# All matrices B of the gates' expansion on VectorE instead of one in four on GpSimd

## The chip, the cores and the metric

The kernel runs on one core of one Trainium2 chip. The metric is the device time of one execution in microseconds (us). The core has a matrix engine (TensorE, PE in the profile, with its weight loads as PEld), VectorE (DVE), ScalarE (ACT), GpSimd (POOL) and SyncE (SP). Each of them works through its own queue of instructions in order, and waits on semaphores for the others. DMAs are issued by SP and, for gathers with an index per row, by POOL.

## The reference, cut to what matters

The block has two mixers side by side (a chunkwise mLSTM and a forgetting attention), an output projection, and then a product-key expert retrieval (PEER) over 16384 experts. It is the last part that the change is in. For each token and each of 8 heads it takes the 16 best of 128 x 128 experts, makes a softmax gate of their scores, and computes

```
u = u_emb[ids]                                   # 128 rows of 1024 for each token
act = gelu(einsum('ted,td->te', u, xb))
w = gate * act
out = einsum('te,ted->td', w, v_emb[ids])
```

So each token has 128 pairs (expert, gate); there are 1024 tokens and 128 experts' rows of u and of v for each of them.

## The kernel before, in words

The 1024 tokens are four segments of 256. The mixers run over the segments one after the other, each merged with the projections of the next segment and the expert choice (`topk`) of earlier ones. The expert sums are computed in two ways:

- **Segments 0 and 3 by gathers.** For each block of 128 tokens, POOL issues one indirect DMA for each of the 128 choices of rows of u (L325, tile `gu`, 128 rows of 4 KB). Each such tile is multiplied with the tokens and summed, on VectorE (L334), or, for 5 of 16 choices, multiplied on POOL (L331) and summed on ScalarE (L332). Then come 128 gathers of v (L361, tile `gv`), one for each token; after every fourth of them TensorE multiplies the four tiles with the gates (L383, `po`). The gathered tiles of segment 0 come from a pool of four buffers (GATH = 4), so a round of four `gv` has to be used by `po` before the next round can be issued. The four blocks' gathers stand in the order u of block 0, then v of block 0 and u of block 1 in turns of four, then v of block 1. For segment 3 they are paced: each is asked for at a fixed place in the dense stage, waits for TensorE's work up to there, and is used five steps later (`Paced`, L1005), so VectorE's, ScalarE's and TensorE's instructions that use it have fixed places among those of the dense stage.
- **Segments 1 and 2 densely.** For 512 tokens the scores with all 16384 experts are made with matmuls (`du` L289), passed through gelu, multiplied with a dense gate matrix and multiplied with all of v (`vo` L1222). Operands of these matmuls are split into a high and a low half: ScalarE casts (`wh` L277), VectorE subtracts (`wl` L282, some of them on POOL, L280, in earlier stages).

The dense gate matrix is made in `gates` (L1091), from the choices of segments 1 and 2, for each of 512 tokens: a matrix A (128 x 128) is one where the high part of a choice's id equals the column, a matrix B is the gate where the low part equals the column, and the product of B and A, a matmul over the 128 choices, is the token's gates for all 16384 experts (`gout` L1136). Tokens are taken four at a time; there are 128 such quads. In a quad, VectorE makes three A with one instruction (L1126), ScalarE the fourth with two (L1129, L1130); then four instructions at L1134 make the four B, then four matmuls, and ScalarE copies the result out of PSUM (L1138). A and B have two buffers each, the PSUM bank two. After eight quads SP writes 2 MB to DRAM (L1140). The line that changes chose POOL for the first B of a quad (GPOOL = 1) and VectorE for the other three.

This expansion is one of three generators that run merged (L1167): the expert choice of segment 3, the last 12 of 48 early blocks of dense scores (`spill`), and the gates. The gathers of segment 0 come later in program order (`gather_first(5)`, L1169), but the framework places each engine's instructions by a simulated timeline when it builds the program, so they stand between the others on POOL, from 383 us on. After the expansion its buffers are given up, and the dense stage takes their place. `po` matmuls and `gout` matmuls both have high priority in that placement. Once built, each engine's order is fixed.

Of the kernel before, what the change touches and what calls it, by code (L numbers as in the profile page):

```python
# [14 lines left out]
OP = mybir.AluOpType  # L15
# [41 lines left out]
SW = 1  # L57
GP0 = 5
GACT = 1
GPOOL = 1  # L60
T3W = 1.2
GW = 1
T00 = 0
# [28 lines left out]
def _block_kernel(ctx, tc, nc, I, out, dbg):  # L92
# [27 lines left out]
    def bank(name):  # L120
        turn_b[0] += 1
        if extra is not None and turn_b[0] % XB == 0:
            return extra[:, turn_b[0] // XB % 2, :]
        return ps.tile([P, 512], F32, tag="bank", name=name, bufs=2)
# [9 lines left out]
    dve, act, pe, pool_e, sync = nc.vector, nc.scalar, nc.tensor, nc.gpsimd, nc.sync  # L134
# [34 lines left out]
    iota = cp.tile([P, P], F32, tag="iota", name="iota")  # L169
# [921 lines left out]
    def gates(S, gb):  # L1091

        for b in range(NB):
            hi = gb.tile([P, P], I32, tag="gi", name="gi_hi")
            lo = gb.tile([P, P], I32, tag="gi", name="gi_lo")
            dve.tensor_scalar(hi, S.idx[:, b, :], 7, None, op0=OP.logical_shift_right)
            dve.tensor_scalar(lo, S.idx[:, b, :], 127, None, op0=OP.bitwise_and)
            T = []
            for x, nm in ((hi, "iT"), (lo, "jT"), (None, "gT")):
                if x is None:  # L1100
                    f = S.gate[:, b, :]
                else:
                    f = gb.tile([P, P], F32, tag="gf", name="gf", bufs=1)
                    dve.tensor_copy(f, x)
                tb = bank("gtr")
                with tc.high_priority():
                    pe.transpose(tb[:, 0:P], f, ident)
                t_ = gb.tile([P, P], F32, tag=nm, name=nm, bufs=1)
                act.copy(t_, tb[:, 0:P])
                T.append(t_)  # L1110
            iT, jT, gT = T
            if GACT:
                niT = gb.tile([P, P], F32, tag="niT", name="niT", bufs=1)
                act.mul(niT, iT, -1.0)
            for tg in range(P // TG):
                G = gb.tile([P, P, TG], F32, tag="G", name="G")
                for q in range(TG // 4):
                    bk = dps.tile([P, 512], F32, tag="db", name="gout")
                    t0 = tg * TG + q * 4
                    ts4 = slice(t0, t0 + 4)  # L1120
                    A = gb.tile([P, 4, P], F32, tag="A", name="A")
                    B = gb.tile([P, 4, P], F32, tag="B", name="B")
                    bc = [P, 4, P]
                    io = iota.unsqueeze(1).broadcast_to(bc)
                    nd = 4 - GACT
                    dve.tensor_tensor(A[:, 0:nd], io[:, 0:nd], iT[:, t0:t0 + nd].unsqueeze(2).broadcast_to([P, nd, P]),  # L1126
                                      op=OP.is_equal)
                    for u in range(nd, 4):
                        act.activation(A[:, u, :], iota, AF.Abs, bias=niT[:, t0 + u:t0 + u + 1])  # L1129
                        act.activation(A[:, u, :], A[:, u, :], AF.Relu, bias=1.0, scale=-1.0)  # L1130
                    for u in range(4):
                        t1 = slice(t0 + u, t0 + u + 1)
                        e = pool_e if u < GPOOL else dve
                        e.tensor_scalar(B[:, u, :], iota, jT[:, t1], gT[:, t1], op0=OP.is_equal, op1=OP.mult)  # L1134
                        with tc.high_priority():
                            pe.matmul(bk[:, u * P:(u + 1) * P], B[:, u, :], A[:, u, :], start=True, stop=True)  # L1136
                    with nullcontext():
                      act.copy(G[:, :, q * 4:q * 4 + 4].rearrange("p i t -> p t i"),  # L1138
                             bk.rearrange("p (t i) -> p t i", t=4))
                sync.dma_start(gd[(NB * (S.sg - DENSE[0]) + b) * (P // TG) + tg], G)  # L1140
                yield
# [21 lines left out]
    def all_gates():  # L1163
        for d in DENSE:
            yield from gates(segs[d], gb)
# [121 lines left out]
```

## Time and profile before

| what | value |
|---|---|
| median of 3 runs | 3746.05 us (3735.21 to 3759.56) |
| the profiled execution's own time | 3742.05 us |
| its span in the profile | 3740.3 us |
| busy share of the span | PE 81%, DVE 69%, POOL 52%, ACT 38% |
| stretch in which L1134 runs | 1699 to 2111 us |
| POOL's instructions at L1134 | 128, mean 1108 ns |
| VectorE's instructions at L1134 | 384, mean 398 ns |

The shares are averages over stages with different limits, so most of what follows is read from stretches of the span: which engine is busy in one, what the others wait for, and which of these waits ends last.

### The profile page before, as it was taken

The numbers are of one execution on the slowest core, as the hardware profiler recorded it, in microseconds if no ns is written. First come the engines' busy times: TensorE is split into PE (matmuls) and PEld (weight loads), VectorE is DVE, ScalarE is ACT, GpSimd is POOL, SyncE is SP. The second block draws the span as 40 slices with busy tenths as digits, with TensorE's granted clock in tenths as the row PEclk, the third lists the DMA queues.
The fourth block names the chain that finished last, engine by engine and source line by source line (L and its number), as shares of the span: only waits on it lengthen the run. The fifth ranks groups of instructions, "written<-read, shape, count | busy, mean of one in ns | idle before, by whom it ended". The sixth has DMA issues, their size and how long they took to land. (4 is left out here: it accounts for less than half of the span.)

```text
span 3740.3 us, 47105 instructions
## 1 busy us (share of the span) xinstructions
PE 3040.7 (81%) x15233; PEld 2324.6 (62%) x15233; DVE 2581.1 (69%) x6272; ACT 1435.7 (38%) x2915; POOL 1944.4 (52%) x1575
## 2 busy tenths in 40 slices
PE   7798776657778889887886599865798888989999
PEld 6686666446556667656765476644576555666667
DVE  6566999987447988888997443877655656654434
ACT  4565443345343323335655432322333332332222
POOL 3121566666545545557656422888655555543430
PEclk9899876768788999988998899887899999999999
DMA  4455577777877778767776777988888788889983
GB/s 140 123 156 166 191 228 243 240 226 250 229 241 238 242 223 257 240 239 263 271 251 234 272 253 248 325 285 287 283 295 293 269 284 290 313 317 328 330 292 109
DMA packets 375899, 931.54 MB, mean 249 GB/s; under 512 B 59316, under 2 KB 145556, under 8 KB 373604
## 3 DMA queue, kind: packets, MB, share of 16 engines
q0 software_dynamic: 161216, 552.56, 44.3%
q1 hardware_dynamic: 214436, 375.97, 30.4%
q8 instruction: 120, 1.97, 0.2%
q14 instruction: 127, 1.04, 0.1%
HBM read 860.91 MB, written 67.47 MB: 248 GB/s over the span
## 5 line engine op out<-in xcount | busy, mean ns | idle before, releaser
L282 DVE TENSOR_TENSOR wl<-raw,wh 128x512 fp32r<-128x512 f32 x736 | 608.4, 833 | 508.6 <-ACT wh L277 455.7
L277 ACT CAST wh<-raw 128x512 fp32r<-128x512 f32 x896 | 543.0, 617 | 971.4 <-DMA raw<-in_peer_v 208.5
L325 POOL DMA_INDIRECT gu<-in_peer_u,idx x512 | 578.9, 1131 | 567.9 <-PE po L383 173.7
L361 POOL DMA_INDIRECT gv<-in_peer_v,idT x512 | 558.2, 1090 | 603.4 <-PE po L383 198.2
L334 DVE SCALAR_TENSOR_TENSOR gu<-gu,xng 128x1024 f32<-128x1024 f32 x352 | 512.8, 1467 | 99.0 <-DMA gu<-in_peer_u,idx 91.9
L1222 PE MATMUL vo<-wh,Wh 128*128 128x512 f32 x1024 | 395.1, 418 | 138.5 <-ACT wh L277 114.0
L1222 PE MATMUL vo<-wl,Wh 128*128 128x512 f32 x1024 | 423.1, 413 | 12.2 <-DVE wl L282 12.1
L331 POOL TENSOR_TENSOR gu<-gu,xng 128x1024 f32<-128x1024 f32 x160 | 389.7, 2436 | 71.8 <-DMA gu<-in_peer_u,idx 66.3
L1222 PE MATMUL vo<-wh,Wl 128*128 128x512 f32 x1024 | 415.8, 408 | 0.0
L280 POOL TENSOR_TENSOR wl<-raw,wh 128x512 fp32r<-128x512 f32 x160 | 217.8, 1361 | 325.9 <-ACT wh L277 294.7
L1222 PEld LDWEIGHTS vo<-wh,Wh 128*128 128x128 f32 x1024 | 198.4, 197 | 231.9 <-ACT wh L277 136.3
L383 PE MATMUL po<-gv,Z 128*32 128x512 f32 x2048 | 273.4, 641 | 78.0 <-DMA gv<-in_peer_v,idT 78.0
L332 ACT ACTIVATE gu<-gu 128x1024 f32<-128x1024 f32 x160 | 169.2, 1058 | 364.6 <-POOL gu L331 357.2
L289 PE MATMUL du<-xh,wh 128*128 128x512 f32 x640 | 259.0, 405 | 30.3 <-ACT wh L277 30.3
L289 PE MATMUL du<-xh,wl 128*128 128x512 f32 x640 | 258.8, 405 | 22.2 <-DVE wl L282 22.1
L289 PE MATMUL du<-xl,wh 128*128 128x512 f32 x640 | 256.2, 400 | 0.0
L1222 PEld LDWEIGHTS vo<-wl,Wh 128*128 128x128 f32 x1024 | 204.0, 199 | 69.9 <-DVE wl L282 19.8
L1222 PEld LDWEIGHTS vo<-wh,Wl 128*128 128x128 f32 x1024 | 203.3, 199 | 51.9 <-issue 6.7
L1136 PE MATMUL gout<-A,B 128*128 128x128 f32 x1024 | 161.3, 310 | 65.1 <-POOL B L1134 51.9
L1136 PEld LDWEIGHTS gout<-A,B 128*128 128x128 f32 x1024 | 146.6, 217 | 93.8 <-POOL B L1134 69.9
L1227 DVE TENSOR_TENSOR acc<-acc,vo 128x512 f32<-128x512 f32 x256 | 164.7, 680 | 47.2 <-PE vo L1222 46.7
L1207 DVE TENSOR_TENSOR Wl<-w,Wh 128x512 fp32r<-128x512 f32 x128 | 96.0, 754 | 133.2 <-ACT Wh L1206 113.5
(431 smaller groups left out, 6696.3 us busy)
## 6 DMA issues: line engine op xcount, KB each, us to landing
raw<-in_ut SPq DMA_DIRECT2D x128, 512.0 KB
raw<-in_peer_v SPq DMA_DIRECT2D x256, 256.0 KB
raw<-in_wf SPq DMA_DIRECT2D x64, 512.0 KB
gd<-G SPq DMA_DIRECT2D x16, 2048.0 KB
Gt<-gd SPq DMA_DIRECT2D x32, 1024.0 KB
raw<-in_wt SPq DMA_DIRECT2D x48, 512.0 KB
raw<-in_wq SPq DMA_DIRECT2D x48, 512.0 KB
raw<-in_wo SPq DMA_DIRECT2D x32, 512.0 KB
```

The source lines that it names most:

```text
L277: act.copy(h, part)
L280: pool_e.tensor_sub(l, part, h.bitcast(F32))
L282: seen["dve"] = dve.tensor_sub(l, part, h.bitcast(F32))
L289: seen["pe"] = pe.matmul(o, w, x[:, c], start=(first and i == 0), stop=(last and i == 2))
L325: d = pool_e.indirect_dma_start(out=t, out_offset=None, in_=I["peer_u"], in_offset=bass.IndirectOffsetOnAxis(ap=S.idx[:, lb, r:r + 1], axi ...
L331: pool_e.tensor_tensor(t, t, xn[0], op=OP.mult)
L332: act.activation(t, t, AF.Copy, accum_out=G.actv[:, r:r + 1])
L334: dve.scalar_tensor_tensor(t, t, 1.0, xn[0], op0=OP.mult, op1=OP.mult, accum_out=G.actv[:, r:r + 1])
L361: d = pool_e.indirect_dma_start(out=t, out_offset=None, in_=I["peer_v"], in_offset=bass.IndirectOffsetOnAxis(ap=S.idT[lb][:, tok:tok + 1], ...
L383: last = pe.matmul(G.po[32 * q_:32 * q_ + 32, n, :], z[:, q_, 31 - j:63 - j], rows[q_][:, n * 512:(n + 1) * 512], start=(j == 0), stop=(j ...
L1136: pe.matmul(bk[:, u * P:(u + 1) * P], B[:, u, :], A[:, u, :], start=True, stop=True)
L1222: seen["pe"] = pe.matmul(bks[b], w[:, cw], v, start=(ii == 0 and i == 0), stop=(ii == GRP - 1 and i == 2))
```

## The change

The constant goes, and with it the choice of the engine: the first B of each quad is made by VectorE too, with the same instruction on the same operands.

```diff
-GPOOL = 1
...
                     for u in range(4):
                         t1 = slice(t0 + u, t0 + u + 1)
-                        e = pool_e if u < GPOOL else dve
-                        e.tensor_scalar(B[:, u, :], iota, jT[:, t1], gT[:, t1], op0=OP.is_equal, op1=OP.mult)
+                        dve.tensor_scalar(B[:, u, :], iota, jT[:, t1], gT[:, t1], op0=OP.is_equal, op1=OP.mult)
```

128 instructions move from POOL's queue to VectorE's. No DMA, no matmul and no buffer is added or taken away.

## Rows read from the trace of the kernel before

**Rows 1.** The page's 40 slices of 93.5 us: busy tenths of PE.
```profile
PE   7798776657778889887886599865798888989999
```
**Rows 2.** Stretches: from:to, length, busy us (instructions) by engine, PE clock, DMA share, GB/s.
```profile
1695.00:1965.00 270.00, 234.91 (x1496) 190.00 (x1500) 249.71 (x907) 158.67 (x322) 182.31 (x153) 0.93 0.72 255
1965.00:2115.00 150.00, 100.73 (x641) 77.87 (x633) 102.21 (x343) 87.54 (x185) 99.14 (x94) 0.85 0.62 230
...
2165.00:2365.00 200.00, 192.42 (x925) 141.19 (x925) 92.88 (x148) 54.90 (x95) 69.93 (x65) 1.00 0.78 265
2365.00:2665.00 300.00, 188.50 (x660) 137.04 (x658) 225.00 (x285) 89.27 (x162) 254.04 (x167) 0.81 0.84 286
```
**Rows 3.** Waits from 2365 to 2665 us: who for whom, total us, times, longest.
```profile
ACT gu L332 <- POOL gu L331: 170.9, 35, 9.2
...
PE vo L1222 <- ACT wh L277: 60.3, 14, 10.7
```
**Rows 4.** POOL's timeline: start, length, instruction (segment 3's first gather).
```profile
2332.28 0.94 POOL L325 DMA_INDIRECT gu<-in_peer_u,idx  x1 [8.89 <-DMA raw<-in_peer_v]
```
**Rows 5.** Stretches, gathers of v at L361 alone: POOL busy us (count), PE clock, DMA.
```profile
1500.00:1695.00 195.00, 34.01 (x29) 0.89 0.76 251
1695.00:1811.00 116.00, 14.68 (x11) 0.90 0.69 245
1811.00:1965.00 154.00, 40.12 (x36) 0.96 0.74 264
1965.00:2115.00 150.00, 37.58 (x36) 0.85 0.62 230
2115.00:2173.00 58.00, 11.55 (x12) 0.79 1.00 335
2173.00:2332.00 159.00, 43.90 (x44) 1.00 0.73 245
```
**Rows 6.** The same stretches, gathers of u at L325 alone.
```profile
1500.00:1695.00 195.00, 28.39 (x28) 0.89 0.76 251
1695.00:1811.00 116.00, 13.62 (x12) 0.90 0.69 245
```
**Rows 7.** The same, matrices B at L1134 alone: DVE busy (count), POOL busy (count).
```profile
1695.00:1811.00 116.00, 32.37 (x84) 36.61 (x30) 0.90 0.69 245
```
**Rows 8.** Groups, 1695 to 2115 us: line, instruction, count | busy us, mean ns | idle before.
```profile
L1134 POOL TENSOR_SCALAR B<-iota,jT,gT 128x128 f32<-128x128 f32 x128 | 141.5, 1108 | 66.9 <-PE gout L1136 51.6 <-ACT gT L1109 11.7 <-POOL B L1134 2.0
...
L1134 DVE TENSOR_SCALAR B<-iota,jT,gT 128x128 f32<-128x128 f32 x384 | 128.9, 398 | 1.1 <-ACT gT L1109 1.1
L361 POOL DMA_INDIRECT gv<-in_peer_v,idT x83 | 92.4, 1113 | 49.2 <-PE po L383 29.1 <-issue 10.9 <-PE gout L1136 4.0
```
**Rows 9.** Waits from 1695 to 2115 us, total us, times, longest.
```profile
PE gout L1136 <- POOL B L1134: 51.9, 26, 5.6
...
DVE A L1126 <- PE gout L1136: 48.3, 30, 5.9
...
DVE gu L334 <- DMA gu<-in_peer_u,idx: 8.5, 3, 4.7
...
DVE Z L377 <- PE po L383: 7.0, 7, 1.8
```
**Rows 10.** POOL's timeline, one round of segment 0's gathers and the next one's start.
```profile
1966.77 1.10 POOL L361 DMA_INDIRECT gv<-in_peer_v,idT  x1 [1.81 <-PE po L383]
...
1972.37 1.63 POOL L1134 TENSOR_SCALAR B<-iota,jT,gT 128x128 f32<-128x128 f32 x2
...
1979.53 1.02 POOL L361 DMA_INDIRECT gv<-in_peer_v,idT  x1 [1.59 <-PE po L383]
```
**Rows 11.** VectorE's timeline: start, length, three B of one quad.
```profile
1988.59 0.93 DVE L1134 TENSOR_SCALAR B<-iota,jT,gT 128x128 f32<-128x128 f32 x3
```
**Rows 12.** Line L361 over the span: duration ns min/median/max, first and last start.
```profile
L361 POOL DMA_INDIRECT gv<-in_peer_v,idT x512: 932/944/3217, 862.1 to 3643.1; - x171
```

## The prediction

> **What bounds the kernel now.** I read the page's slices first: PE is at eight or nine tenths almost everywhere after 1000 us, with two dips, slices 21 and 22 (1964 to 2151 us) and slices 26 to 28 (2431 to 2712 us) [rows 1]. The change sits in the first. The stretches then show what each dip is made of [rows 2]. From 1695 to 1965 VectorE is the full one (250 of 270 us); from 1965 to 2115 no engine is (PE 101, DVE 102, POOL 99 of 150). In the second dip, 2365 to 2665, POOL is busy 254 of 300 us, while PE makes 660 instructions in 300 us after 925 in 200: at the earlier rate, 4.6 per us, those 660 take 143 us, so 157 us are lost there, 111.5 of them plain idle.
>
> The waits of the second dip name the chain [rows 3]: ScalarE waits 171 us for POOL's multiplication of a gathered tile, and behind it in ScalarE's queue stand the casts for which TensorE waits. These are the gathers of segment 3, asked for at fixed places of the dense stage, and they are late. Why: POOL gets to the first of them only at 2332 us [rows 4], 217 us into the dense stage, because the last 56 gathers of segment 0 (12 + 44 [rows 5]) stand ahead of it in the queue.
>
> So the end hangs on a chain on POOL: the time S (now 2332) at which segment 0's gathers are through. What S gains the lost 157 us give back, one for one, until they are used up. When the gates' stretch itself ends (2115) hardly matters: an earlier dense stage would only wait longer in the second dip.
>
> What paces segment 0's gathers? Count them by stretch [rows 5, 6]. Before the gates: 29 + 28 in 195 us, 3.42 us each. At the start of the gates, 1695 to 1811: 11 + 12 in 116 us, 5.04 each. Then gathers of v alone: 36 + 36 in 304 us, 4.22 each. After the gates, 2173 to 2332: 44 in 159 us, 3.61 each. They are slowest exactly where matrices B share their queue.
>
> **The change, part by part.**
>
> *Off POOL:* 128 instructions, 141.5 us busy, behind which POOL stood a further 66.9 us waiting, 51.6 of them for a B buffer that TensorE had not freed [rows 8]. What was queued behind that wait is the gathers.
>
> First stretch, 1695 to 1811: 23 gathers at 5.04 instead of 3.42 us are 37 us too many, and the 30 B in it take 36.6 us of POOL [rows 7], the same size. Bounds: 0 and 37 us. It lies nearest the upper one by POOL's row, but VectorE, which sums most of the u tiles, is also nearly full here, and it gets more work; I take 25.
>
> Second stretch, 1811 to 2115: 72 gathers at 4.22 instead of 3.61 us are 44 us. Bounds: 0 and 44. Here one round shows how little of B is in the way [rows 10]: first gather at 1966.77, next round at 1979.53, and the B in between stand after the fourth gather, while the data are still on their way and POOL has nothing else to do. What B costs a round is then indirect: TensorE waits for POOL's B 51.9 us in the gates [rows 9], and `po`, which frees the round's four buffers, stands behind that wait in TensorE's order. With 18 rounds in the stretch I take 15 us, a third of the upper bound.
>
> S comes 25 + 15 = 40 us earlier, to about 2292.
>
> *Onto VectorE:* three B in a row take 0.93 us, 0.31 each [rows 11]; 128 x 0.31 = 40 us (by the stretch's mean of 0.398 [rows 8] it would be 51). VectorE is busy 352 us of the 420 from 1695 to 2115 [rows 2], and idle 68, of which 48.3 are its A waiting for a `gout` matmul [rows 9], which in turn waited for POOL's B. That wait is the cover: with it gone, 352 + 40 + about 20 for the waits that stay (8.5 for a gather, 7.0 for `po`, and small ones [rows 9]) is 412 of 420 us. So I cost it at nothing. Without that cover it costs 40 us, which is the third rival.
>
> *Waits:* none is added. VectorE already waits for the same buffers at A; a quad's matmuls wait for one engine less. No DMA moves; what POOL's queue loses lets the splits at L280 and the gathers go earlier; SP's transfers of G follow the quads, and nothing in the dips waits for them. Before the first B nothing should change.
>
> *Sum:* 3742 (the profiled execution's own time) - 40 = 3702 us. The median shown is 4 us above that execution, so the prediction is **3706 us**.
>
> **A rule against the change.** In the trace a gather's issue at L361 takes 0.944 us at the median, 1.113 in the gates [rows 8, 12], and up to 3.2 [rows 12]. The excess here is 0.17 us for each of 95 gathers; four B where there were three would add at most a third of it, 5 us. The Trainium skill (SBUF — State Buffer, Who interferes with whom) says that a VectorE `tensor_scalar` can take the port pair it shares with GpSimd for the whole instruction, and that GpSimd then can't write the descriptors of its gathers; it gives about 620 ns alone and 3100 beside such work. By those figures 95 gathers, each hit once more, would be an estimated 236 us later. The trace agrees with its direction, and hardly with its size: the mean is far from the maximum.
>
> **The rivals.**
> - *More of the same:* all rounds go at the shortest cycle, 12.76 us [rows 10]. 18 rounds then take 230 instead of 304 us, 74 less, and with the full 37 of the first stretch S falls by 111, within the 157 that can be given back: 3746 - 111 = 3635. For it: every B leaves the queue. Against: most rounds' cycle is landing time, during which the DMA engines are already 0.62 to 0.74 busy [rows 5].
> - *No change:* gathers are held by fixed places of `po` among the `gout` matmuls, by landing, and by VectorE; B only filled POOL's pauses, as in the round shown. S stays: 3746, 20 us either way, since all orders after 1695 are made anew. Against it: the 5.04 us per gather.
> - *VectorE becomes the bound of the gates, slower:* if its A goes on waiting 48 us for `gout` (now behind other TensorE work), the 40 us of B come on top of 420, `po` stands behind later `gout` matmuls, and S moves by the same 40: 3786; 3797 by the longer mean. It decides once VectorE's idle time stays near 68 us. For it: 93% busy from 1695 to 1965, where by time 270/420 of the 40 us, 26, meet only 20 idle. Against: from 1965 to 2115 it has 48 us to spare.
> - *Gathers starved:* each quad's extra B catches a gather's issue. If one in four of the 95 takes the longest 3.2 us, that is 24 x 2.1 = 50 us: 3796. It is the rule above; the means speak against it.
>
> That the change doesn't do what it says I leave out: the engine of each of these instructions is in the code.
>
> **How the numbers follow.** Forecast 0.45, more of the same 0.13, no change 0.20, VectorE's bound 0.18, starved 0.04. The forecast's own range is its bounds with VectorE's risk: 3746 - 81 = 3665 to 3736. A measurement of this kernel can tell about 1% from no change, 37 us. Faster by over that: 0.6 of the forecast (its lower bound lies further off than its upper) and all of the second, 0.27 + 0.13 = 0.40. Slower by over that: three quarters of VectorE's bound and the starved case, 0.135 + 0.04, 0.18. The rest, 0.42, is within 1%. The range takes in the forecast, no change, about half of the second case and a third of the third: 3640 to 3775.
>
> **What would show it.** At L1134 VectorE has 512 instructions, POOL none, and TensorE's 52 us of waiting for POOL there are gone. VectorE's A waits far less than 48 us for `gout`, and the gates end near 2115. POOL's first gather for segment 3 starts near 2292, with the gain already 25 us at the last gather of u of segment 0. In the second dip ScalarE's wait of 171 us for POOL and PE's lost time shrink by as much as S moved, and the end moves with them. Wrong in the mechanism: S earlier and the end not, or the end earlier with S in place. Wrong in the size: S moves by under 10 us or later. If VectorE is over 97% busy through the gates and `gout` waits for its B, the third rival holds.

## The result: 0.7% slower, and the profile after

Median 3769.61 us after, 3741.75 before, over 16 runs of each; the ratio, from which executions in a slower state are left out, is 1.0073, interval 1.0055 to 1.0091. The prediction was 3706 and its range 3640 to 3775: the time is in the range, but the change made the kernel slower where a faster one was forecast. The profiled execution has a span of 3765.2 us, 24.9 over the one before. Single executions of one kernel lie up to 1% apart here, so traces are compared below by stretches, and kernels by the ratio.

The edit does what it says. The source line of B after it (durations min/median/max, first and last start), and its group in the gates' stretch (count | busy us, mean ns | idle before):

```profile
L1132 DVE TENSOR_SCALAR B<-iota,jT,gT x512: 320/341/2407, 1704.8 to 2131.9; 128x128 f32<-128x128 f32 x171
```
```profile
L1132 DVE TENSOR_SCALAR B<-iota,jT,gT 128x128 f32<-128x128 f32 x512 | 162.4, 380 | 0.0
...
L360 POOL DMA_INDIRECT gv<-in_peer_v,idT x90 | 95.9, 1066 | 212.7 <-PE po L382 186.3 <-PE gout L1134 8.4 <-issue 6.5
```

(Lines count one less above the edit and two less below it.) VectorE's B took 128.9 us and takes 162.4, 33.5 more. POOL has no B; its 141.5 busy and 66.9 waiting us at B [rows 8] have turned into 186.3 us of waiting for `po` at the gathers of v (29.1 before).

Now the end of segment 0's gathers, on POOL's timeline (start, length, instruction): the last gather of v and segment 3's first gather.

```profile
2340.64 0.95 POOL L360 DMA_INDIRECT gv<-in_peer_v,idT  x1 [0.30 <-issue]
2358.49 0.94 POOL L324 DMA_INDIRECT gu<-in_peer_u,idx  x1 [16.90 <-DVE Wl L1205]
```

S is 2358.5, where before it was 2332.3 [rows 4]: 26.2 us later, and the span is 24.9 longer. S is not quite the time at which segment 0's gathers are through: the last gather of v is 18.2 us later (2322.45 before), and the other 8 us are the first gather's own wait. It starts 8.8 us after the end of segment 0's last `po` (0.3 before), and the trace puts the wait down to VectorE's `Wl`, an instruction of the dense stage. The second dip is the old one moved by as much. Stretches of the kernel after (from:to, length, busy us (instructions) of PE, PEld, DVE, ACT, POOL, clock, DMA share, GB/s), the gates and the dip shifted by 25 us:

```profile
1700.00:2141.00 441.00, 343.06 (x2149) 260.00 (x2149) 372.33 (x1379) 251.30 (x505) 145.36 (x126) 0.89 0.68 241
```
```profile
2390.00:2690.00 300.00, 195.64 (x659) 141.13 (x658) 224.08 (x276) 88.09 (x159) 257.50 (x168) 0.78 0.84 286
```

659 PE instructions in the dip, 660 before [rows 2]. So the end moved with S, and S went the wrong way. But the end of the gates moved by just as much, from 2113.3 to 2139.5 us (the last `gout` before, as duration and first and last start; the one after is in TensorE's timeline below):

```profile
L1136 PE MATMUL gout<-A,B x1024: 270/275/583, 1701.2 to 2113.0; 128*128 128x128 f32 x171
```

So these two traces alone can't tell which of the two the end follows. Why the gates grew is in the waits of their stretch (who for whom, total us, times, longest):

```profile
DVE Z L376 <- PE po L382: 46.9, 9, 11.1
...
PE po L382 <- DMA gv<-in_peer_v,idT: 42.6, 12, 10.0
...
PE gout L1134 <- DVE B L1132: 25.5, 32, 2.2
...
DVE A L1125 <- PE gout L1134: 6.3, 9, 1.7
```

Read them against [rows 9]. TensorE's 51.9 us for POOL's B are gone, and VectorE's 48.3 at A have become 6.3, as forecast. But VectorE now waits 46.9 us at Z (7.0 before): Z is the small copy of a gates' column without which the next `po` can't start, and it can't be made before the `po` two rounds earlier has read its buffer. And TensorE waits 42.6 us for gathers to land (9.5 before), and 25.5 us for VectorE's B (2.5 before). VectorE's idle time is 441 - 372.3 = 69 us, as it was; its 20 us of net added busy time came on top. From the first transpose of the gates to the last `gout` it was 416 us and is 437.

The gathers by stretch, v alone and then u (POOL busy, count), 5 us later than [rows 5, 6] because this execution reached the gates 5.3 us later:

```profile
1700.00:1816.00 116.00, 16.27 (x15) 0.90 0.74 265
1816.00:1970.00 154.00, 35.27 (x33) 0.90 0.66 234
1970.00:2139.00 169.00, 42.46 (x41) 0.88 0.64 230
```
```profile
1700.00:1816.00 116.00, 11.93 (x12) 0.90 0.74 265
```

In the first stretch 27 gathers instead of 23: 4.30 us each, not 5.04. So far the forecast holds: the last u gather came 92 us after the first gates' transpose, not 104. But then 74 in 323 us, 4.36 each, where it was 4.22. Of the 12 us, 11 were lost within one round: the round issued at 1806.3 got its successor only at 1840.3, 34 us later (23 before). Its `po` stands behind the `gout` of 35 quads in the order of the new program, behind 32 in the old one, and comes 18.4 us after its tiles have landed (7.2 before). That round's successor is 6 us behind its twin of before (1834.1), and the rounds that follow take 4 us of that back: the one issued at 2157.4 is 2 us behind (2155.4). A second loss is at the start of the dense stage. TensorE's timeline after, from the last `gout`:

```profile
2138.69 0.85 PE L1134 MATMUL gout<-A,B 128*128 128x128 f32 x3
2153.55 3.60 PE L382 MATMUL po<-gv,Z 128*32 128x512 f32 x16 [14.01 <-DMA gv<-in_peer_v,idT]
2170.89 0.79 PE L1220 MATMUL vo<-wh,Wh 128*128 128x512 f32 x1 [13.74 <-ACT Wh L1204]
...
2182.39 1.92 PE L382 MATMUL po<-gv,Z 128*32 128x512 f32 x16
```

The gates end later, so the first dense matmul starts later, at 2171 (2142 before), and a round whose tiles had landed 13.6 us earlier waits with its `po` behind 43 dense matmuls. In the old order that lateness was 1.4 us, after one of 7.4 in the round before. The next round is issued at 2184.6, 11 us behind its twin (2173.5); the ten rounds after it lose 7 more, and the wait before segment 3's first gather the last 8. So in these two traces nearly all of S's 26 us is lost not in the gates but behind them, where the dense stage starts 29 us later.

### The profile page after: what moved, and what is told of

Read it like the earlier page. It is cut to its first block, busy times and chain, and to the rows that moved or that the text cites. A ratio compares the mean times of both kernels' runs of the same rounds, so it can differ in the third digit from the quotient of the medians.

```text
span 3765.2 us, 46895 instructions
## 1 busy us (share of the span) xinstructions
PE 3055.9 (81%) x15233; PEld 2323.3 (62%) x15233; DVE 2603.5 (69%) x6400; ACT 1443.6 (38%) x2915; POOL 1807.1 (48%) x1447
## 5 line engine op out<-in xcount | busy, mean ns | idle before, releaser
L281 DVE TENSOR_TENSOR wl<-raw,wh 128x512 fp32r<-128x512 f32 x736 | 593.4, 813 | 532.6 <-ACT wh L276 500.0
L382 PE MATMUL po<-gv,Z 128*32 128x512 f32 x2048 | 282.7, 663 | 111.8 <-DMA gv<-in_peer_v,idT 111.4
L382 PEld LDWEIGHTS po<-gv,Z 128*32 128x32 f32 x2048 | 57.1, 116 | 241.8 <-DMA gv<-in_peer_v,idT 119.9
L1134 PE MATMUL gout<-A,B 128*128 128x128 f32 x1024 | 159.1, 296 | 37.9 <-DVE B L1132 25.5
L1134 PEld LDWEIGHTS gout<-A,B 128*128 128x128 f32 x1024 | 139.3, 201 | 78.8 <-issue 28.6
```

Of the source, the lines that this page charges most:

```text
L281: seen["dve"] = dve.tensor_sub(l, part, h.bitcast(F32))
L382: last = pe.matmul(G.po[32 * q_:32 * q_ + 32, n, :], z[:, q_, 31 - j:63 - j], rows[q_][:, n * 512:(n + 1) * 512], start=(j == 0), stop=(j ...
```

## The experiments

Theory A: VectorE's added work lengthens the gates. Theory B: POOL's freed queue changed the order. Theory S: the end follows S. Four kernels came first, then four built on their answers, then a control and a candidate.

**e1_none and e2_both: the two halves of the change.** In e1 nobody makes the first B; in e2 both engines make it.

```diff
-                    for u in range(4):
+                    for u in (1, 0, 2, 3):
...
-                        dve.tensor_scalar(B[:, u, :], ...)
+                        if u:
+                            dve.tensor_scalar(B[:, u, :], ...)
-                            pe.matmul(..., B[:, u, :], A[:, u, :], ...)
+                            pe.matmul(..., B[:, max(u, 1), :], A[:, u, :], ...)
```


> Leaves out the first B of each quad: nobody makes it, VectorE makes three as before, and the first matmul of a quad takes the second B. So GpSimd has no B and VectorE no added work. Theory A (VectorE's added 40 us of work make the gates' stretch longer, and that is the loss): ratio to the kernel before 0.990 to 1.000, the gates end some 20 us earlier than after the change. Theory B (what costs is the order that the program gets once GpSimd's queue is free of B: rounds of gathers stand closer among the quads, TensorE waits for their landing, 43 us instead of 9.5): ratio 1.004 to 1.008, as after the change, with those waits still there.

```diff
                         e.tensor_scalar(B[:, u, :], ...)          # the kernel before
+                        if u == 0:
+                            spare = gb.tile([P, P], F32, tag="spare", name="spare")
+                            dve.tensor_scalar(spare, iota, jT[:, t1], gT[:, t1], ...)
```


> The kernel before, and VectorE makes the first B a second time into a spare tile that nobody reads: GpSimd's B stays, and VectorE has the added work. Theory A (VectorE's added work): ratio to the kernel before 1.006 to 1.010. Theory B (order after GpSimd's queue is freed): 0.998 to 1.002, TensorE's wait for GpSimd's B still near 50 us.

e1: ratio 1.0007 (0.9987 to 1.0026). e2: 1.0038 (1.0013 to 1.0062). VectorE's 128 instructions cost 0.38% where POOL keeps its own (e2 against before) and 0.66% where it does not (after against e1). Freeing POOL costs nothing measurable without them. That is mainly theory A; e2 is about halfway, so A alone doesn't give the size. In e1's trace the gates' stretch is 388 us instead of 416 and S is 7 us earlier (POOL's timeline, segment 3's first gather), while the median is that of the kernel before:

```profile
2325.26 0.94 POOL L324 DMA_INDIRECT gu<-in_peer_u,idx  x1 [16.71 <-PE du L288]
```

This would say that a shorter stretch is worth nothing as long as S stays. The trace doesn't show it: the traced execution is the fastest of its twelve, 25 us under their median, and in it the end comes 22 us earlier than in the trace before, with the gates' end 30 us earlier.

**e3_pool_spare: VectorE's work, with POOL's queue full as before.**

```diff
+                        if u == 0:
+                            spare = gb.tile([P, P], F32, tag="spare", name="spare")
+                            pool_e.tensor_scalar(spare, iota, jT[:, t1], gT[:, t1], ...)
                         dve.tensor_scalar(B[:, u, :], ...)          # the kernel after
```


> The kernel after, and GpSimd makes the first B once more into a spare tile that nobody reads and that waits for no matmul: VectorE makes all four B, GpSimd's queue is as full of instructions as before. Theory A (VectorE's added work): ratio to the kernel before 1.006 to 1.010, as after the change or worse. Theory B (order after GpSimd's queue is freed): near 1.000, since the gathers stand among the same instructions again.

1.0019 (0.9993 to 1.0045), below A's range and near 1.000, as theory B expected. But B is refuted by e1. So neither holds alone: with VectorE carrying all four B, instructions on POOL that nothing else needs take most of the loss away, and with POOL's queue empty (e1) three B on VectorE cost nothing. Here VectorE waits for `po` at Z much less than the 46.9 us after the change (waits in its gates' stretch):

```profile
DVE Z L376 <- PE po L382: 18.5, 4, 7.7
```

**e4_s_early: S earlier, by rounds left out.**

```diff
-               for j in range(32) for q in range(4)]
+               for j in range(32) if not (S.sg == 0 and lb == 1 and 16 <= j < 24) for q in range(4)]
```


> The kernel after, with 8 of the last 16 rounds of segment 0's v gathers left out (32 gathers and their matmuls, part of that segment's sums). Theory S (the end follows the time at which segment 0's gathers are through on GpSimd): 8 rounds of 14.6 us, 117 us, come off that time and off the end: about 3653 us, ratio to before 0.97 to 0.98, the second dip much smaller. Rival (the end follows the end of the gates and TensorE's work): only the matmuls left out, 8 x 1.9 = 15 us: about 3755, ratio 1.003.

3692.93 us, 0.9867 (0.9834 to 0.9901), 77 us under the kernel after. S went from 2358.5 to 2236.5, 122 us:

```profile
2236.51 0.94 POOL L324 DMA_INDIRECT gu<-in_peer_u,idx  x1 [25.70 <-DMA out_dram<-h2o]
```

The matmuls left out are an estimated 15 us (8 rounds of 1.9) and the gates ended 11 us earlier, so the rival is out; but the end gained at most 0.63 of what S did, less than expected. The order up to the rounds left out is that of the kernel after, and the two losses recur: lateness of 16.5 us in the round of 1804 (18.4 after) and 13.8 at the dense start (13.6).

**e5_z_pool and its control e9_z_pool_before: Z on POOL.**

```diff
-            dve.tensor_copy(z[:, :, 31:32], G.wT[:, :, j:j + 1])
+            (pool_e if S.sg == 0 else dve).tensor_copy(z[:, :, 31:32], G.wT[:, :, j:j + 1])
```


> The kernel after, with segment 0's copies Z (the gates' column for the next round of po, now on VectorE, 47 us of waiting for po in the gates' stretch instead of 7) made on GpSimd, which is free there and waits for po anyway. Theory C (VectorE's idle time was no cover: it went over from A's wait to Z's wait): VectorE's wait for po in the gates nearly gone, the gates' stretch 437 us shorter by 20 or more, ratio to the kernel before 0.998 to 1.004. Rival (TensorE's own waits for the landing of gathers bound the gates, whoever makes Z): the stretch stays near 430, ratio 1.005 to 1.009.

> The kernel before, with segment 0's copies Z on GpSimd, the control to the same edit of the kernel after. Theory C (it helped the kernel after because there VectorE had come to wait 47 us for po at Z): the kernel before waits only 7 us there, so ratio to it 0.997 to 1.003, and with GpSimd's B still in the queue rather above 1. Rival (Z on GpSimd is good for any of these kernels, whoever makes B): 0.989 to 0.994, as it gained 0.9% on the kernel after.

e5: 0.998 (0.9963 to 0.9997), 35 us under the kernel after: the whole loss is back, and all of B still on VectorE. e9: 1.0005 (0.9977 to 1.0033): the same edit does nothing where POOL makes a B. In e5 VectorE has no Z to wait at; a part of the wait goes back to A, where it was before the change. TensorE still waits for landing (both lines from 1700 to 2125 us, 27 us past the end of this kernel's gates; inside them TensorE's wait is 32.0 us):

```profile
DVE A L1125 <- PE gout L1134: 38.7, 11, 9.8
```
```profile
PE po L382 <- DMA gv<-in_peer_v,idT: 51.0, 15, 16.0
```

VectorE's idle time in the stretch fell from 67 to 43 us, the stretch from 437 to 420, a little less than the 20 expected, and S to 2293. The edit also let the gates begin some 20 us earlier, in both kernels (1678), so this part isn't what separates them. One rival stays: e5 gives POOL instructions again, as e3 does, and e3 took most of the loss away with Z still on VectorE. No run takes Z off VectorE without adding to POOL.

**e6_gact2: less work on VectorE by another way.**

```diff
-GACT = 1
+GACT = 2
```


> The kernel after, with the third A of each quad made by ScalarE too (two instructions, some 0.7 us) and only two by VectorE. Theory A (VectorE's work): VectorE's A falls from 0.58 to about 0.42 us, 20 us in all, half of what the change put on it; ratio to the kernel before 1.000 to 1.004. Rival (ScalarE, 251 us busy and 90 more, delays its copies out of PSUM and with them the matmuls): ratio 1.006 or more.

1.0054 (1.0031 to 1.0077), between the two expectations. VectorE's busy time from the first transpose to the last `gout` fell from 370 to 358 us, and that stretch from 437 to 423, but S stayed at 2359 and the ratio nearly so; its interval overlaps that of the change, so whether the edit gains anything isn't clear. (The traced execution ends 10.6 us before that of the kernel after, with the gates' end 11.6 us earlier.)

**e7_more_after and e8_more_before: rounds that overlap.** Four more gather buffers in memory free from the gates on, for every second round of segment 0's last 32; the same edit on both kernels.

```diff
+    more.append(pool("gmore", 4, gbs, reuse_waits="tile"))
...
-            t = gp.tile([P, D], F32, tag="g", name="gv")
+            two = S.sg == 0 and lb == 1 and tok % 32 % 2 and more
+            t = (more[0] if two else gp).tile([P, D], F32, tag="g", name="gv")
```


> The kernel after, with four more gather buffers in the memory that is free from the gates on, used by every second round of the last 32 rounds of segment 0, so that a round can be gathered while the one before is used. Theory S (the end follows the time at which segment 0's gathers are through): rounds of 16.4 us overlap, that time comes 100 us earlier or more, and the end 60 to 80 (leaving out 8 rounds gave 77 for 122): ratio to the kernel before 0.980 to 0.990. Rival (landing and TensorE's waits for it stretch the gates by as much): 1.000 to 1.010.

> The kernel before, with the same four more gather buffers. Theory S: ratio to the kernel before 0.975 to 0.985, and if B on VectorE is harmful for its work, lower than the same with the kernel after by 0.004 to 0.007. Rival (landing): 0.995 to 1.005.

e7: 3668.35 us, 0.9805 (0.9774 to 0.9836). e8: 3690.49 us, 0.9889 (0.985 to 0.9927), short of its expectation. Segment 3's first gather in e7, and e7's stretches where the dip was:

```profile
2145.84 0.95 POOL L326 DMA_INDIRECT gu<-in_peer_u,idx  x1 [2.61 <-PE po L385]
```
```profile
2165.00:2365.00 200.00, 159.28 (x620) 123.99 (x621) 158.67 (x205) 70.11 (x125) 125.78 (x81) 0.87 0.81 268
2365.00:2665.00 300.00, 265.88 (x1139) 209.66 (x1138) 216.23 (x296) 107.67 (x188) 181.48 (x121) 0.94 0.80 272
```

1139 PE instructions where there were 660 to 672: the dip is gone from there. A smaller one has come before it, 620 in the 200 us where there were 925 [rows 2]; in both stretches together it is 1759 instead of 1585. And the sign of the change has turned. With the rounds overlapped, B on VectorE is 0.8% faster than B on POOL (0.9805 to 0.9889). The traces give a likely reason: S now stands only 36 and 26 us behind the gates' end, the gates take 413 us in e7 and 448 in e8 (first transpose to last `gout`), and in e8 TensorE still waits for POOL's B:

```profile
PE gout L1139 <- POOL B L1137: 34.2, 15, 5.3
```

**e10_more_z_pool: a version that beats both.** The kernel after with both edits.

> The kernel after, with the four more gather buffers and segment 0's copies Z on GpSimd, as a candidate to beat both kernels. Theory S and C together: the second dip is already small with the buffers, so the end now follows the gates' end; VectorE still waited 31 us for po at Z there; without that the gates are 10 to 30 us shorter: ratio to the kernel before 0.973 to 0.980. Rival (landing of the gathers bounds the gates then): 0.980 to 0.985, as with the buffers alone.

3641.33 us, 0.9714 (0.9668 to 0.9759): 2.9% under the kernel before, better than expected, but not for the expected reason. The 31 us at Z were read from a stretch that reached 40 us past the end of e7's gates; inside them VectorE waits 2.4 us there. In e10 the gates are 9 us shorter than in e7 and begin 21 us earlier, as they do in e5 and e9. The dip's stretch in it:

```profile
2365.00:2665.00 300.00, 273.98 (x1195) 213.68 (x1194) 216.55 (x300) 107.23 (x187) 178.47 (x123) 0.95 0.81 278
```

All of them: the ratio from all runs, and from the one trace of each its span, S, the end of the gates (last `gout`) and their length (from the first transpose):

| kernel | ratio to before | span, us | S, us | gates' end, us | gates, us |
|---|---|---|---|---|---|
| before | 1 | 3740 | 2332 | 2113 | 416 |
| after | 1.0073 | 3765 | 2358 | 2140 | 437 |
| e1, no first B | 1.0007 | 3719 | 2325 | 2083 | 388 |
| e2, both make it | 1.0038 | 3779 | 2355 | 2149 | 444 |
| e3, spare B on POOL | 1.0019 | 3767 | 2347 | 2125 | 421 |
| e4, 8 rounds left out | 0.9867 | 3689 | 2237 | 2128 | 425 |
| e5, Z on POOL | 0.998 | 3733 | 2293 | 2098 | 420 |
| e6, GACT = 2 | 1.0054 | 3755 | 2359 | 2128 | 423 |
| e7, more buffers | 0.9805 | 3674 | 2146 | 2110 | 413 |
| e8, more buffers, before | 0.9889 | 3689 | 2168 | 2142 | 448 |
| e9, Z on POOL, before | 1.0005 | 3730 | 2350 | 2096 | 418 |
| e10, more buffers and Z | 0.9714 | 3641 | 2136 | 2079 | 404 |

The ratios go with S better than with the gates' length (e1, e2, e6), though not one for one: e9 has S 18 us later at no cost. The spans say something else. In the eight kernels with four buffers and all rounds, a span is the gates' end plus 1626 to 1642 us, while S stands anywhere from 195 to 254 us behind that end. Four of the traced executions lie 11 to 25 us off the median of their kernel (e1, e2, e3, e9), so for shifts of this size it stays open which of the two the end follows. That S counts is shown where it moved far towards the gates' end: in e4, e7, e8 and e10, where it stands 26 to 108 us behind it, the distance from there to the end of the span is 1546 to 1564 us.

## Why the prediction was wrong, step by step

- **What bounds the kernel: right in part.** That the late gathers of segment 3 cost time, and that an earlier S gives some of it back, was confirmed by e4, e7 and e8. "One for one" was too much for a gain: e4 gave at most 0.63, e7 101 us of end for 213 of S against the kernel after, 0.48. That the gates' end "hardly matters" is not borne out: in the change it moved by as much as S, and the spans go with it.
- **First stretch, 25 us: right in kind, half in size.** 12 us at the last u gather, counted from the gates' start.
- **Second stretch, 15 us: wrong.** The step says that TensorE's wait for POOL's B is what keeps `po` late. The wait went, and TensorE waits for landing instead, 42.6 us; the rounds stayed at 16.4 us on average through the gates (16.5 before).
- **VectorE's work costed at nothing: the step that failed.** "That wait is the cover: with it gone, 352 + 40 + about 20 for the waits that stay (...) is 412 of 420 us." The 40 was nearly right (33.5). The wait at A went as said. But the waits that stay didn't stay: Z's went from 7.0 to 46.9 us, so idle time remained 69 and the gates grew by 21. e5 and e9 speak for this wait: made elsewhere, Z gives the loss back, and only in the kernel that has it (with the rival named at e5: its order).
- **From there to S.** Longer gates reach S through fixed places in the order: a `po` behind more `gout`, another behind dense matmuls that start later, and segment 3's first gather behind an instruction of the dense stage. The first of these left the gathers 2 us late at the start of the dense stage; the rest of the 26 came behind it. This is read from the traces of the change, and for the two `po` from e4; no run moved such a place by itself.
- **The rivals.** "VectorE becomes the bound" came true by its criterion, idle time that stays near 68 us, at 28 us instead of 40; it named A for the wait, and it was Z. The other sign given for it did not come: VectorE is 84% busy through the gates (372.3 of 441 us), not over 97%. So VectorE did not bound them by being full; it stood idle as long as before, at another instruction. The starved gathers did not come: with four B a gather's issue takes 1.066 us, not more than the 1.113 of before [rows 8]. The Trainium skill's rule (SBUF — State Buffer, Who interferes with whom), by which such VectorE work holds up the writing of descriptors, doesn't show in this mean; an effect hidden under POOL's own B having left isn't excluded. The 620 and 3100 ns that the prediction took with it the Trainium skill gives (SBUF — State Buffer, A bandwidth-pool intuition that's wrong (but worth ruling out)) for a DMA beside a VectorE `tensor_copy`, not a `tensor_scalar`.
- **The range.** That it holds the measured time is not to the forecast's credit: it was widened for rivals, and its centre lies on the other side of no change. The 3736 us at which the forecast's own range ends is not worked out; with both gains at nothing it would be 3746.
- **Open:** whether the loss reaches the end by S or by the gates' end, and why e2 and e3 lie between. Each build has another order of all engines after the first gate; what an order is worth by itself no run shows.

## What to carry to other kernels

A wait that a change removes is cover for new work only if nothing else is queued to take its place: list what stands next in the waiting engine's order, and what that depends on. When the end hangs on a chain of rounds, ask first what limits one round (here four buffers, refilled only after the last use); freeing an engine that the round didn't need gave nothing here (e1). Then retry the edits that failed: with rounds overlapped, this same change gains 0.8%.

## What the runs showed of the hardware beyond that

VectorE's splits at L282, two tiles read per instruction, took 818 ns on the mean in the gates before and 680 after. In the trace before, those beside a multiply or subtraction of two tiles on POOL took 1.5 to 2.8 us, those beside a B on POOL 0.68, as alone. So B on POOL didn't slow these splits, and the four long ones all ran beside POOL's two-input work. That doesn't always catch them: in the trace after, three splits beside a subtraction on POOL took 0.68 to 0.69 us. VectorE's own B was a little slower beside POOL's B, 367 ns on the mean against 335 alone.
